# The first stage of a hybrid decoder layer: identity, silu, row sums and two bias rows rearranged

## The chip, the cores and the metric

The kernel runs on one core of a Trainium2 chip. Its engines are TensorE (PE, with its weight loads as PEld), VectorE (DVE), ScalarE (ACT), GpSimd (POOL) and SyncE (SP), which here only issues DMAs. The metric is the device time of one execution in microseconds. Changes of 0.3% and less can hardly be told from none.

## What is computed

One decoder layer on 256 tokens of 1024 features, all in float32. `c` is one row of 1024, `ada_w` is 1024 x 6144.

```python
mod = silu(c) @ ada_w + ada_b
sh1, sc1, gt1, sh2, sc2, gt2 = split(mod, 6)
h = rmsnorm(x, norm1_g) * (1 + sc1) + sh1
x = x + gt1 * hybrid_mixer(h)          # w_in: 1024 x 6144, RG-LRU and gMLP branches, merged, w_out
h = rmsnorm(x, norm2_g) * (1 + sc2) + sh2
x = x + gt2 * moe(h)                   # router: 32 experts, top 4; clamped SwiGLU experts of 1024
out = rmsnorm(x, final_g)
```

In the gMLP branch the weights `w_s` (8 groups, 128 x 128) are used as lower triangles, and a bias row `b_s` is added; the router adds `b_router`.

## The kernel before, in words

**Loads.** SBUF holds 24 slots of 128 x 2048 floats, 1 MB each. All large weights stream through them in one list of loads, which SP issues in order: `pump` issues the next load when a slot is free, `give` frees one. At most eight of SP's loads are in flight, since a load waits for the one eight before it. The list begins with the pieces of `ada_w` for `sh1` and `sc1` ("a1", six pieces: feature blocks 0, 1, 2-3, 4-5, 6, 7 as `PIECES` says) in turn with the blocks of `w_in` that go with them ("w"). Then come the rest of the mixer's weights with 16 loads of `ada_w` for the other four parts ("a2"), then 12 MB for each of 32 experts. Behind the load ("w", 6), the hook `small_loads` puts four small loads into the queue: the row `b_s` (4 KB, to one partition), the row `b_router` (128 bytes, to one partition), `w_s` and the LRU gate weights.

**Products.** All products of the mixer are made from float32 split in two parts: `split(u)` takes half a slot, ScalarE copies it rounded (the high part, line 259), and POOL or VectorE subtracts to get the low part (line 263; `ON_POOL` says which). Units 1 to 10 are subtracted on POOL, 0, 11, 12 and 14 on VectorE, and later on odd ones on POOL, even ones mostly on VectorE. `product(u)` then runs 24 matmuls: high x high, high x low part of the activations, low x high. After unit 11 the splits run four units ahead of the products.

**The first stage.** Constants first: POOL makes the identity (line 212), the strict triangle `lt` (line 215), a ramp `iota` (line 218) and clears `selX` (line 239). The rows of x are normalized into `xh` (lines 226 to 230). silu of c is made from a tanh (lines 234 to 236) and put into the columns of `selX` (`cz`). Then `transposes` turns all of xh with 16 TensorE transposes into four banks and copies these to `xT`. For each piece, `ada_rows(i)` sums the piece's `ada_w` rows weighted by silu(c): pieces 0, 1, 4, 5 (`ROWS_ON_PE`) by eight matmuls of 32 output rows on TensorE and one copy, pieces 2 and 3 by eight operations on VectorE of 128x512 (lines 339 and 341). `ada_cols(i)` finishes the sum with small matmuls against ones and adds the bias columns; `modulate(i)` applies shift and scale to xT and splits the result into `hh` and `hl`, the activations of every product. Pieces and products take turns in the order that the lines behind `n_steps = len(chunks)` write out by hand; each engine takes its instructions in that order.

**Further on.** After unit 13, `lower_triangles` masks the eight `w_s` blocks on POOL, then spreads the two bias rows to all partitions with `partition_broadcast` (lines 375 and 378), which is a custom instruction of POOL. Convolution, gates, scan and gating follow beside the products of steps 6 to 33, mainly on VectorE and ScalarE, and the 16 "a2" loads are accumulated on VectorE (lines 399 and 401). Then the router, and 32 experts one after the other.

The first pieces in the order that is written out by hand:

```python
transposes()
drop("xh")
ada_rows(0)
ada_cols(0)
split(0)
modulate(0)
```

## Time and profile before

| what | us |
|---|---|
| median of 3 runs | 1290.69 |
| lowest, highest | 1287.26, 1291.13 |
| the profiled execution | 1289.19 |
| its span in the profile | 1287.5 |
| PE busy (6667 matmuls) | 1199.5 |
| DVE busy | 554.8 |
| ACT busy | 256.7 |
| POOL busy (80 instructions) | 143.8 |

The profile holds one execution. The span runs from the first instruction to the last. The page cuts it in 40 equal slices and gives the busy share of each engine in tenths, PEclk, the granted TensorE clock in tenths of full speed, and what the DMA engines moved. The timeline lists instructions in order of time; in brackets behind a row stands how long its engine was idle before it and what released it. "issue" means that the profile shows nothing for which it waited. The windows give busy time by engine over chosen stretches.

### The profile page before, as it was taken

To read this page: it belongs to the slowest core of one execution; us is meant where nothing else is said; L and a number is where in the kernel's file an instruction comes from. 1 tells how busy PE (TensorE), PEld (TensorE's weight loads), DVE (VectorE), ACT (ScalarE), POOL (GpSimd) and SP (SyncE) were. 2 spreads that over 40 slices of the span, in tenths; PEclk is the share of its full clock that TensorE was granted. 3 is DMA by queue.
4 is the path that set the end of the run, shared out by engine and by line. 5 is a ranking of instruction groups with operands and counts; after the bars stand their busy time and mean duration, and the time that the engine had idled before them with its cause. 6 is when DMAs were issued, how large, how long until landed. Compare 5 with 4: busy or idle time off the path is not lost. (4 is left out here: it accounts for less than half of the span.)

```text
span 1287.5 us, 17398 instructions
## 1 busy us (share of the span) xinstructions
PE 1199.5 (93%) x6667; PEld 633.9 (49%) x6667; DVE 554.8 (43%) x993; ACT 256.7 (20%) x474; POOL 143.8 (11%) x80
## 2 busy tenths in 40 slices
PE   5797889999999999999999999999999999998996
PEld 4796888986444443444444444443433333433442
DVE  4586998665233333333333333333333333334324
ACT  3264633443111111111111111111111111101112
POOL 2443645531000000000000000000000000000010
PEclk8898999999999999999999999999999999999998
DMA  9964526978999999999999999999999999999960
GB/s 372 419 273 168 230 100 228 404 290 330 362 418 417 416 404 417 419 418 418 419 419 419 418 418 419 418 418 415 414 414 416 415 414 412 418 412 419 412 244 35
DMA packets 66582, 472.94 MB, mean 367 GB/s; under 512 B 7577, under 2 KB 7705, under 8 KB 10308
## 3 DMA queue, kind: packets, MB, share of 16 engines
q1 hardware_dynamic: 66100, 470.13, 89.6%
q8 instruction: 114, 1.87, 0.6%
q14 instruction: 96, 0.79, 0.2%
q0 software_dynamic: 272, 0.16, 0.0%
HBM read 469.21 MB, written 1.05 MB: 365 GB/s over the span
## 5 line engine op out<-in xcount | busy, mean ns | idle before, releaser
L268 PE MATMUL bank<-gu,gv 128*64 128x512 f32 (+1 forms) x2112 | 471.3, 597 | 13.4 <-DMA gu<-in_w_gu 7.7
L268 PEld LDWEIGHTS bank<-gu,gv 128*64 128x64 f32 (+1 forms) x2112 | 144.9, 136 | 300.1 <-issue 258.1
L268 PE MATMUL bank<-dn,tmp 128*64 128x512 f32 (+3 forms) x1120 | 240.9, 580 | 1.1 <-ACT tmp L983 0.3
L268 PEld LDWEIGHTS bank<-dn,tmp 128*64 128x64 f32 (+1 forms) x1120 | 72.5, 136 | 133.6 <-issue 119.1
L268 PEld LDWEIGHTS bank<-selX,x 128*128 128x128 f32 x1024 | 118.4, 193 | 39.4 <-DVE tmp L969 38.3
L268 PE MATMUL bank<-selX,x 128*128 128x128 f32 x1024 | 124.6, 280 | 12.1 <-PEq L1221 12.1
L995 DVE TENSOR_REDUCE wsl<-bank 128x1 f32<-128x256 f32 x33 | 14.0, 425 | 279.4 <-PE bank L994 279.4
L263 POOL TENSOR_TENSOR parts<-w,parts 128x1024 fp32r<-128x1024 f32 x40 | 117.9, 2956 | 116.7 <-ACT parts L259 83.5
L268 PE MATMUL bank<-hh,parts 128*128 128x256 f32 x640 | 122.2, 301 | 8.7 <-DVE parts L263 4.5
L970 ACT ACTIVATE tmp<-tmp 128x512 f32<-128x512 f32 (+1 forms) x34 | 20.8, 610 | 458.1 <-DVE tmp L969 458.1
L268 PEld LDWEIGHTS bank<-hh,parts 128*128 128x128 f32 x640 | 104.1, 206 | 12.3 <-DVE parts L263 4.9
L1253 POOL DMA_DIRECT2D selX<-in_rows x4 | 2.2, 545 | 952.8 <-PE bank L268 952.8
L1013 DVE TENSOR_TENSOR h<-bank,h 128x512 f32<-128x512 f32 x124 | 79.5, 683 | 47.4 <-PE bank L268 47.4
L268 PE MATMUL bank<-hl,parts 128*128 128x256 f32 x320 | 85.8, 299 | 0.0
L999 DVE SCALAR_TENSOR_TENSOR tmp<-bank,wsl,gt2h 128x512 f32<-128x512 f32 x31 | 23.3, 750 | 126.5 <-PE bank L268 126.5
L259 ACT ACTIVATE parts<-w 128x1024 fp32r<-128x1024 f32 x66 | 67.3, 1052 | 50.1 <-POOL parts L263 14.6
L827 DVE TENSOR_SCALAR gv<-bank,ab 128x128 f32<-128x128 f32 x128 | 43.7, 404 | 70.4 <-PE bank L268 70.4
L1001 ACT ACTIVATE on<-tmp 128x512 fp32r<-128x512 f32 x31 | 19.5, 630 | 263.0 <-DVE tmp L999 263.0
L268 PEld LDWEIGHTS bank<-hl,parts 128*128 128x128 f32 x320 | 62.2, 210 | 0.2 <-issue 0.2
L829 ACT ACTIVATE gv<-bank,ab 128x128 f32<-128x128 f32 x128 | 48.2, 457 | 65.6 <-PE bank L268 65.6
L263 DVE TENSOR_TENSOR parts<-w,parts 128x1024 fp32r<-128x1024 f32 x32 | 44.4, 1395 | 29.0 <-ACT parts L259 28.9
L969 DVE TENSOR_SCALAR tmp<-bank 128x512 f32<-128x512 f32 (+1 forms) x34 | 22.7, 668 | 68.0 <-PE bank L268 67.8
(228 smaller groups left out, 999.2 us busy)
## 6 DMA issues: line engine op xcount, KB each, us to landing
gu<-in_w_gu SPq DMA_DIRECT2D x256, 1024.0 KB, 19.8
dn<-in_w_dn SPq DMA_DIRECT2D x124, 1024.0 KB, 19.9
w<-in_mix SPq DMA_DIRECT2D x32, 1024.0 KB, 8.0
a<-in_mix SPq DMA_DIRECT2D x24, 1024.0 KB, 8.0
w<-in_mix SPq DMA_DIRECT2D x8, 512.0 KB, 16.3
dn<-in_w_dn_last SPq DMA_DIRECT2D x4, 768.0 KB, 19.8
x<-in_x SPq DMA_DIRECT2D x2, 512.0 KB, 4.2
wab<-in_lru_w SPq DMA_DIRECT2D x1, 1024.0 KB, 11.2
```

The source lines that it names most:

```text
L259: nc.scalar.activation(hi, w, AF.Copy)
L263: (nc.gpsimd if u in ON_POOL else nc.vector).tensor_tensor(lo, w, hi.bitcast(F32), op=OP.subtract)
L268: nc.tensor.matmul(o, a, b, start=start, stop=stop, skip_group_check=True)
L827: nc.vector.tensor_scalar(dst, src, ab[:, 1, k:k + 1], ab[:, 0, k:k + 1], op0=OP.mult, op1=OP.add)
L829: nc.scalar.activation(dst, src, AF.Identity, bias=ab[:, 0, k:k + 1], scale=ab[:, 1, k:k + 1])
L969: nc.vector.tensor_scalar(gcl, g, LIMIT, None, op0=OP.min)
L970: nc.scalar.activation(sig, gcl, AF.Sigmoid, scale=ALPHA)
L995: nc.vector.tensor_reduce(w, T[:, :256], axis=mybir.AxisListType.X, op=OP.add)
L999: nc.vector.scalar_tensor_tensor(osb, o, w, g, op0=OP.mult, op1=OP.mult)
L1001: nc.scalar.activation(dst[0], osb, AF.Copy)
L1013: nc.vector.tensor_tensor(xa[:, b, c], C[h], xa[:, b, c], op=OP.add)
L1253: nc.gpsimd.dma_start(frow[q], rows[R_FG:R_FG + 1, q * 256:(q + 1) * 256])
```

## The change

- The identity is made by VectorE: a ramp along the row by a scan, its 32x32 blocks transposed, and the two compared on the four diagonal blocks. The ramp is `iota`, so POOL no longer makes that one, nor clears selX. POOL keeps `lt`.
- `colt`, with c and the bias columns, is loaded ahead of x. silu of c and what hangs on it come ahead of the normalization. ScalarE so loads its tanh table first and its square root table second.
- `ada_rows(0)` comes ahead of the transposes, which are cut in four by bank: bank 0, then split, columns and modulation of piece 0, then banks 1 to 3. The split of unit 0 comes ahead of `ada_cols(0)`.
- All six pieces are summed by TensorE. The sums go to bank 7 for pieces 1 and 5, to bank 6 for the others.
- The two bias rows are loaded to all 128 partitions by SP's DMAs (512 KB and 16 KB). The three partition broadcasts are gone.

```diff
--- before.py
+++ after.py
@@ -35,7 +35,6 @@
 HI_ON_DVE = {27, 28, 29, 30, 31, 33}
 
 PIECES = ((0,), (1,), (2, 3), (4, 5), (6,), (7,))
-ROWS_ON_PE = (0, 1, 4, 5)
 
 GROUPS = ("ga", "gb", "va", "vb", "ua", "ub", "gra", "grb", "gsa", "gsb")
 COL0 = {"ga": 1024, "gb": 1536, "va": 3072, "vb": 3584, "ua": 2048, "ub": 2560,
@@ -160,18 +159,18 @@
     want(("dn", E - 1, 4), w_dn_last[:, 16 * WA:])
 
 
+    colt = t([128, N_COLS], "colt")
+    nc.sync.dma_start(colt, cols)
     xv = view(new("x"), TB)
     for b in range(TB):
         nc.sync.dma_start(xv[:, b], x[b * 128:(b + 1) * 128])
-    colt = t([128, N_COLS], "colt")
-    nc.sync.dma_start(colt, cols)
     R["tmp"] = new("tmp")
     tmp = [R["tmp"][:, i * 512:(i + 1) * 512] for i in range(4)]
     tms = [tmps.tile([128, 512], F32, name=f"tms{i}", tag="tmp") for i in range(2)]
     gt2h = t([128, 512], "gt2h")
     secure("xh", "xT", "wab", "ws", "acc")
     lg, mask, wt, posm = (t([128, TB, E], n) for n in ("lg", "mask", "wt", "posm"))
-    brow = wt[0:1, 0]
+    brb = t([128, E], "brb")
     gv = t([128, D], "gv")
     two = t([128, 64], "two", F32R)
     own = [t([128, 128], f"own{i}", F32R) for i in range(2)]
@@ -183,8 +182,8 @@
     wr = selX.rearrange("p (k e) -> p k e", k=KB)
 
     def small_loads():
-        nc.sync.dma_start(R["ws"][0:1, 1024:], rows[R_BS:R_BS + 1])
-        nc.sync.dma_start(brow, b_router)
+        nc.sync.dma_start(gv, rows[R_BS:R_BS + 1].to_broadcast([128, D]))
+        nc.sync.dma_start(brb, b_router.to_broadcast([128, E]))
         nc.sync.dma_start(R["ws"][:, :1024], sg_ws)
         nc.sync.dma_start(R["wab"], lru_w)
 
@@ -206,18 +205,33 @@
     ones, lt = (o.bitcast(F32) for o in own)
     iota = t([128, 128], "iota")
     eps = t([128, 1], "eps")
-    nc.vector.memset(tmp[2][:, :128], 1.0)
+    one = tmp[2][:, :128]
+    nc.vector.memset(one, 1.0)
+    nc.vector.memset(ident, 0.0)
     nc.vector.memset(eps, EPS)
-    nc.vector.tensor_copy(own[0], tmp[2][:, :128])
-    nc.gpsimd.affine_select(ident, tmp[2][:, :128], pattern=[[-1, 128]], compare_op=OP.is_equal, fill=0.0,
-                            base=0, channel_multiplier=1)
-
-    nc.gpsimd.affine_select(tmp[3][:, :128], tmp[2][:, :128], pattern=[[1, 128]], compare_op=OP.is_gt, fill=0.0,
-                            base=0, channel_multiplier=-1)
-    nc.gpsimd.tensor_copy(own[1], tmp[3][:, :128])
-    nc.gpsimd.iota(iota, pattern=[[1, 128]], base=0, channel_multiplier=0, allow_small_or_imprecise_dtypes=True)
+    nc.vector.memset(selX, 0.0)
+    nc.scalar.activation(tmp[3][:, :1], eps, AF.Tanh)
+    nc.vector.tensor_tensor_scan(iota, one, one, -1.0, op0=OP.mult, op1=OP.add)
+
+    nc.vector.transpose(tmp[1][:, :128], iota)
+    for r in range(4):
+        d = slice(32 * r, 32 * r + 32)
+        nc.vector.tensor_tensor(ident[d, d], tmp[1][d, d], iota[d, d], op=OP.is_equal)
+    nc.vector.tensor_copy(own[0], one)
 
     wsT = R["ws"][:, 1024:].rearrange("p (g t) -> p g t", g=8)
+
+
+    cs = t([128, 8], "cs")
+    nc.scalar.activation(cs, colt[:, C_C:C_C + 8], AF.Tanh, scale=0.5)
+    nc.vector.scalar_tensor_tensor(cs, cs, 1.0, colt[:, C_C:C_C + 8], op0=OP.add, op1=OP.mult)
+    nc.vector.tensor_scalar(cs, cs, 0.5, None, op0=OP.mult)
+    cz = selX.rearrange("p (k m) -> p k m", k=8)
+    nc.vector.tensor_copy(cz[:, :, 0], cs)
+
+    ab = t([128, 2, 8], "ab")
+    nc.vector.tensor_copy(ab[:, 0], colt[:, C_AB:C_AB + 8])
+    nc.vector.tensor_scalar(ab[:, 1], colt[:, C_AB + 8:C_AB + 16], 1.0, None, op0=OP.add)
 
 
     st = t([128, 8], "st")
@@ -230,18 +244,9 @@
         nc.vector.tensor_scalar(xh[:, b], xv[:, b], st[:, 4 + b:5 + b], None, op0=OP.mult)
 
 
-    cs = t([128, 8], "cs")
-    nc.scalar.activation(cs, colt[:, C_C:C_C + 8], AF.Tanh, scale=0.5)
-    nc.vector.scalar_tensor_tensor(cs, cs, 1.0, colt[:, C_C:C_C + 8], op0=OP.add, op1=OP.mult)
-    nc.vector.tensor_scalar(cs, cs, 0.5, None, op0=OP.mult)
-
-    cz = selX.rearrange("p (k m) -> p k m", k=8)
-    nc.gpsimd.memset(selX, 0.0)
-    nc.vector.tensor_copy(cz[:, :, 0], cs)
-
-    ab = t([128, 2, 8], "ab")
-    nc.vector.tensor_copy(ab[:, 0], colt[:, C_AB:C_AB + 8])
-    nc.vector.tensor_scalar(ab[:, 1], colt[:, C_AB + 8:C_AB + 16], 1.0, None, op0=OP.add)
+    nc.gpsimd.affine_select(tmp[3][:, :128], one, pattern=[[1, 128]], compare_op=OP.is_gt, fill=0.0,
+                            base=0, channel_multiplier=-1)
+    nc.gpsimd.tensor_copy(own[1], tmp[3][:, :128])
 
 
     parts = {}
@@ -311,37 +316,30 @@
 
     xT = view(R["xT"], 8)
 
-    def transposes():
-        for b in range(TB):
-            for kb in range(KB):
-                nc.tensor.transpose(B[kb // 2][:, (kb % 2) * 256 + b * 128:(kb % 2) * 256 + b * 128 + 128],
+    def transposes(p):
+        for kb in (2 * p, 2 * p + 1):
+            for b in range(TB):
+                nc.tensor.transpose(B[p][:, (kb % 2) * 256 + b * 128:(kb % 2) * 256 + b * 128 + 128],
                                     xh[:, b, kb * 128:(kb + 1) * 128], ident)
-        for p in range(4):
-            dst, src = xT[:, 2 * p:2 * p + 2], B[p].rearrange("p (k s) -> p k s", k=2)
-            if p % 2:
-                nc.vector.tensor_copy(dst, src)
-            else:
-                nc.scalar.activation(dst, src, AF.Copy)
+        dst, src = xT[:, 2 * p:2 * p + 2], B[p].rearrange("p (k s) -> p k s", k=2)
+        if p % 2:
+            nc.vector.tensor_copy(dst, src)
+        else:
+            nc.scalar.activation(dst, src, AF.Copy)
 
     g1 = t([128, 2, 8], "g1")
 
     def ada_rows(i):
 
         n = len(PIECES[i])
-        y, rk = tmp[i % 2][:, :256 * n], B[6 + i % 2][:, :256 * n]
+        y, rk = tmp[i % 2][:, :256 * n], B[7 if i in (1, 5) else 6][:, :256 * n]
         for j in range(n):
             v = view(where["a1", i, j], 8 // n)
             for kk in range(8 // n):
                 k = j * 4 + kk
-                if i in ROWS_ON_PE:
-                    mm(rk[32 * (k % 4):32 * (k % 4) + 32], cz[:, k], v[:, kk], k < 4, k >= 4)
-                elif k:
-                    nc.vector.scalar_tensor_tensor(y, v[:, kk], cs[:, k:k + 1], y, op0=OP.mult, op1=OP.add)
-                else:
-                    nc.vector.tensor_scalar(y, v[:, kk], cs[:, k:k + 1], None, op0=OP.mult)
+                mm(rk[32 * (k % 4):32 * (k % 4) + 32], cz[:, k], v[:, kk], k < 4, k >= 4)
             give()
-        if i in ROWS_ON_PE:
-            nc.scalar.activation(y, rk, AF.Copy)
+        nc.scalar.activation(y, rk, AF.Copy)
 
     def ada_cols(i):
 
@@ -365,17 +363,12 @@
     hh, hl = view(R["hh"], 8), view(R["hl"], 8)
 
     bsb = gv
-    brb = t([128, E], "brb")
 
     def lower_triangles():
         for h in range(2):
             for g in range(4):
                 nc.gpsimd.affine_select(wsn[h][:, g], wsn[h][:, g], pattern=[[-1, 128]], compare_op=OP.is_ge,
                                         fill=0.0, base=0, channel_multiplier=1)
-        nc.gpsimd.partition_broadcast(brb, brow)
-        for h in range(2):
-            c = slice(h * 512, (h + 1) * 512)
-            nc.gpsimd.partition_broadcast(bsb[:, c], R["ws"][0:1, 1024:][:, c])
 
     def spatial_weights():
         for h in range(2):
@@ -696,12 +689,14 @@
             mm_t(u, bo[g], k0, f, l, hh, hl, **kw)
 
     n_steps = len(chunks)
-    transposes()
+    ada_rows(0)
+    transposes(0)
+    split(0)
+    ada_cols(0)
+    modulate(0)
+    for p in range(1, 4):
+        transposes(p)
     drop("xh")
-    ada_rows(0)
-    ada_cols(0)
-    split(0)
-    modulate(0)
 
     def cols(i):
         ada_cols(i)
```

Where this moves instructions (names with a number are tiles: bank6 is a PSUM bank, a1_2_0 the first load of piece 2, parts0 the split of unit 0, own0 the ones, selX the columns of silu(c)).

TensorE at the start of the program, before:

```order
L317 MATMUL bank0_69<-ident_126,xh_86 128x128 x2
L317 MATMUL bank1_70<-ident_126,xh_86 128x128 x2
L317 MATMUL bank2_71<-ident_126,xh_86 128x128 x2
L317 MATMUL bank3_72<-ident_126,xh_86 128x128 x2
L317 MATMUL bank0_69<-ident_126,xh_86 128x128 x2
L317 MATMUL bank1_70<-ident_126,xh_86 128x128 x2
L317 MATMUL bank2_71<-ident_126,xh_86 128x128 x2
L317 MATMUL bank3_72<-ident_126,xh_86 128x128 x2
L268 MATMUL bank6_75<-a1_0_0_102,selX_99 32x256 x8
L268 MATMUL bank7_76<-own0_97,tmp_82 128x1 x2
L268 MATMUL bank7_76<-a1_1_0_106,selX_99 32x256 x8
```

and with the change:

```order
L273 MATMUL bank6_75<-a1_0_0_103,selX_100 32x256 x8
L322 MATMUL bank0_69<-ident_127,xh_86 128x128 x4
L273 MATMUL bank7_76<-own0_98,tmp_82 128x1 x2
L322 MATMUL bank1_70<-ident_127,xh_86 128x128 x4
L322 MATMUL bank2_71<-ident_127,xh_86 128x128 x4
L322 MATMUL bank3_72<-ident_127,xh_86 128x128 x4
L273 MATMUL bank7_76<-a1_1_0_107,selX_100 32x256 x8
```

The sums of piece 0 come first, four transposes stand ahead of the small matmuls that read the sums, and twelve behind them.

VectorE around the sums of piece 2, before:

```order
L359 TENSOR_SCALAR tmp_82<-xT_87,g1_155 128x256
L363 TENSOR_TENSOR hl_101<-tmp_82,hh_100 128x256
L341 TENSOR_SCALAR tmp_82<-a1_2_0_111,cs_146 128x512
L339 SCALAR_TENSOR_TENSOR tmp_82<-a1_2_0_111,cs_146,tmp_82 128x512 x3
L339 SCALAR_TENSOR_TENSOR tmp_82<-a1_2_1_113,cs_146,tmp_82 128x512 x4
L354 TENSOR_TENSOR g1_155<-bank7_76,ab_152 128x2x2
```

TensorE in the same place with the change, behind the small matmuls of piece 1:

```order
L273 MATMUL bank7_76<-own0_98,tmp_82 128x1 x2
L273 MATMUL bank6_75<-a1_2_0_112,selX_100 32x512 x4
L273 MATMUL bank6_75<-a1_2_1_114,selX_100 32x512 x4
L273 MATMUL bank0_69<-hh_101,parts1_225 128x256 x2
L273 MATMUL bank1_70<-hh_101,parts1_225 128x256 x2
```

The eight operations left VectorE; eight matmuls of 32x512 stand on TensorE ahead of product 1, whose operands are parts1.

POOL from the split of unit 13 on, before:

```order
L263 TENSOR_TENSOR parts13_638<-w_6_222,parts13_638 128x1024
L263 TENSOR_TENSOR parts15_658<-w_7_269,parts15_658 128x1024
L263 TENSOR_TENSOR parts17_734<-w_8_275,parts17_734 128x1024
L373 AFFINE_SELECT ws_89<-ws_89 128x128 x8
L375 ISA
L375 ISA brb_156<-wt_93 128x32
L378 ISA gv_95<-ws_89 128x512 x2
L263 ISA
L263 TENSOR_TENSOR parts19_819<-w_9_332,parts19_819 128x1024
```

and with the change:

```order
L268 TENSOR_TENSOR parts13_646<-w_6_228,parts13_646 128x1024
L268 TENSOR_TENSOR parts15_666<-w_7_275,parts15_666 128x1024
L268 TENSOR_TENSOR parts17_742<-w_8_281,parts17_742 128x1024
L370 AFFINE_SELECT ws_89<-ws_89 128x128 x8
L268 TENSOR_TENSOR parts19_824<-w_9_339,parts19_824 128x1024
```

The rows named ISA are configuration changes and custom instructions. Between the triangles and the split of unit 19 none is left.

## Rows read from the trace of the kernel before

**Rows 1.** The page's 40 slices of the span: DMA's busy tenths, and GB/s.
```profile
DMA  9964526978999999999999999999999999999960
GB/s 372 419 273 168 230 100 228 404 290 330 362 418 417 416 404 417 419 418 418 419 419 419 418 418 419 418 418 415 414 414 416 415 414 412 418 412 419 412 244 35
```

**Rows 2.** Timeline, 10 to 20 us: start, duration, engine, operation, count [idle before].
```profile
10.32 3.67 PE L317 MATMUL bank<-ident,xh 128*128 128x128 f32 x16 [10.32 <-POOL ident L212]
13.18 0.69 DVE L322 COPY xT<-bank 128x512 f32<-128x512 f32 x1 [1.47 <-PE bank L317]
13.92 1.94 PE L268 MATMUL bank<-a,selX 128*32 128x256 f32 x16
17.22 1.07 PE L268 MATMUL bank<-a,selX 128*32 128x256 f32 x16 [0.25 <-DVE g L354]
17.29 1.23 DVE L263 TENSOR_TENSOR parts<-w,parts 128x1024 fp32r<-128x1024 f32 x1
19.34 2.07 PE L268 MATMUL bank<-hh,parts 128*128 128x256 f32 x8 [1.05 <-ACT hh L361]
```

**Rows 3.** Timeline, 25 to 53 us, of TensorE and VectorE.
```profile
25.77 1.80 PE L268 MATMUL bank<-hh,parts 128*128 128x256 f32 x8 [1.48 <-ACT hh L361]
26.60 9.47 DVE L339 SCALAR_TENSOR_TENSOR tmp<-a,cs,tmp 128x512 f32<-128x512 f32 x7
36.13 1.69 PE L268 MATMUL bank<-own,tmp 128*128 128x1 f32 x8 [4.29 <-DVE tmp L339]
40.34 11.52 DVE L339 SCALAR_TENSOR_TENSOR tmp<-a,cs,tmp 128x512 f32<-128x512 f32 x7
51.91 1.05 PE L268 MATMUL bank<-own,tmp 128*128 128x1 f32 x8 [2.93 <-DVE tmp L339]
```

**Rows 4.** Line 339 (VectorE's row sums): durations in ns, minimum, median, maximum.
```profile
L339 DVE SCALAR_TENSOR_TENSOR tmp<-a,cs,tmp x14: 750/752/2774, 26.6 to 51.1; 128x512 f32<-128x512 f32 x14
```

**Rows 5.** Windows: length; busy PE, PEld, DVE, ACT, POOL; PEclk, DMA share, GB/s.
```profile
26.10:29.50 3.40, 3.40 (x19) 3.40 (x17) 3.33 (x4) 1.51 (x2) 2.76 (x1) 0.50 1.01 419
36.30:43.10 6.80, 6.80 (x33) 6.80 (x34) 4.94 (x9) 3.58 (x5) 2.64 (x1) 0.50 1.03 422
53.70:56.60 2.90, 2.90 (x16) 2.90 (x15) 1.19 (x4) 2.76 (x5) 0.99 (x1) 0.50 1.00 412
101.60:111.60 10.00, 6.21 (x15) 4.91 (x16) 3.83 (x3) 3.21 (x5) 7.43 (x3) 0.51 0.06 26
101.95:116.62 14.67, 11.23 (x37) 9.10 (x38) 4.78 (x4) 6.93 (x12) 9.09 (x3) 0.68 0.18 60
128.70:181.30 52.60, 44.37 (x328) 41.48 (x326) 51.82 (x52) 29.99 (x43) 31.32 (x12) 0.94 0.49 181
```

**Rows 6.** Timeline of POOL, 80 to 110 us.
```profile
84.28 3.01 POOL L373 TENSOR_SCALAR_AFFINE_SELECT ws<-ws 128x128 f32<-128x128 f32 x8
94.11 0.31 POOL L375 PARTITION_BROADCAST brb<-wt  x1 [6.82 <-issue]
103.00 4.67 POOL L263 TENSOR_TENSOR parts<-w,parts 128x1024 fp32r<-128x1024 f32 x2 [7.22 <-issue]
```

**Rows 7.** Timeline of TensorE, at 105 and 176 us.
```profile
105.39 0.79 PE L268 MATMUL bank<-parts,hh 128*128 128x512 f32 x1 [7.13 <-POOL parts L263]
176.81 0.58 PE L268 MATMUL bank<-ws,v 128*128 128x128 f32 x1 [4.35 <-DVE ws L410]
```

**Rows 8.** Line 122: two loads, to landing; first split of the second.
```profile
L122 SPq DMA_DIRECT2D a<-in_mix x1: 432/432/432, 2.2 to 2.2; - x1
DMA to landing us min/median/max: 7.2/7.2/7.2
L122 SPq DMA_DIRECT2D w<-in_mix x1: 328/328/328, 29.7 to 29.7; - x1
DMA to landing us min/median/max: 16.3/16.3/16.3
71.86 3.89 ACT L259 ACTIVATE parts<-w 128x1024 fp32r<-128x1024 f32 x4
```

## The prediction

> **What bounds the kernel now.** I read the page's slices first, then the timeline by engine of the mixer, then windows over the stretches that stood out. The slices, 32 us each, show two programs: from the eleventh on the DMA engines are at 9 tenths of their time or more and stay there until the last two; before that they are full for two slices and sag to 6, 4, 5, 2 and 6 tenths in the third to seventh, so there the transfers wait for slots, and slots wait for the mixer's chain [rows 1]. Whatever the mixer saves before about 200 us therefore lets all later weight loads start earlier, and comes off the end in full. Transfer engines that idle for half of five slices have room to be asked earlier.
>
> Within the mixer three things stop TensorE. First, nothing runs on it until 10.32 us, when POOL's identity is ready; the sums of piece 0 start only after the 16 transposes, at 13.92 us, and its product at 19.34 us [rows 2]. Second, the row sums of pieces 2 and 3 run on VectorE for 9.47 and 11.52 us, and TensorE waits 4.29 and 2.93 us for them; it also waits 1.48 us at 25.77 us for the first modulated block [rows 3]. One such sum of 128x512 takes 0.75 us at the median and 2.77 us at the worst [rows 4]; the long ones are those beside a POOL subtraction, which is why 7 of them take 9 to 11 us. Behind each wait the granted clock is at its lower level, 0.50: for 3.40, 6.80 and 2.90 us [rows 5]. Third, at 84.28 us POOL does the eight triangles, 3.01 us, and then three partition broadcasts, with 6.82 us of "issue" before the first and 7.22 us before its next subtraction at 103.00 [rows 6]. The subtraction it owes is late, TensorE waits 7.13 us until 105.39 us [rows 7], and from 101.60 to 111.60 us the clock stands at 0.51 while TensorE is busy for 6.21 us [rows 5].
>
> **The change, part by part.** *The start.* The weights of piece 0 are asked for at 2.2 us and land 7.2 us later, at 9.4 us [rows 8]. VectorE makes the identity, zeroes selX and writes cs into it while the loads are on their way: fourteen operations, none over 128x256, so each under half of the 0.69 us that a copy of 128x512 takes [rows 2], 5 us at most. ScalarE has its part of cs early, as colt is now the first load. So the sums run at 9.4 us instead of 13.92. Their 1.94 us end at 11.4. Four of 16 transposes that take 3.67 us follow (0.9), then a copy of one bank (0.7) and what lies in before between the end of the sums, 15.86, and the product, 19.34 us: 3.5 us, with the subtraction of 1.23 us in it, which stays on VectorE ahead of the modulation [rows 2]. That gives 16.5 us. But the product writes four banks, and VectorE now copies two of them to xT only behind the modulation: a subtraction of 0.4 and two copies of 0.69 us [rows 2], so the last bank is free at 18.3 us. The start is worth 1.0 us; 0 to 2.8 are its ends. [...]
>
> *The row sums.* 4.29 and 2.93 us of waiting go, 7.2 in all [rows 3]. Their place takes 16 matmuls of 32x512. Eight of 32x256 take 1.07 us the second time [rows 2], so eight of twice the width take some 2.15, and two pieces 4.3 us. They stand where TensorE waited for the modulated block, so the 1.48 us at 25.77 us are filled too [rows 3]. With no wait of several microseconds left between 18 and 76 us, I take it that the three stretches at half the clock go with the waits ahead of them: half of 3.40 + 6.80 + 2.90 us, or 6.55 [rows 5]. Sum: 7.2 + 1.5 + 6.55 - 4.3 = 10.9 us, with the start 12 us. If none of the clock comes back it is 5.4; with the best start it is 14. The data is there: the weights of the step behind all six sums are asked for at 29.7 us, land 16.3 us later, at 46.0, and ScalarE first splits them at 71.86 us [rows 8], after this change at about 60.
>
> *The copies and the tables.* ScalarE gets two copies of 128x512 out of PSUM, each a copy like the 0.69 us one [rows 2]; they stand behind two and three splits, while TensorE has 36 and 72 matmuls of products in front of the copies' readers. Nothing for them; without those products each would cost its 0.7 us. VectorE loses 21 us of sums; what was queued behind them there, the modulation, now waits for TensorE instead.
>
> *The broadcasts.* POOL gets back what lies between the triangles' end and its next subtraction, 103.00 - 87.29 = 15.7 us [rows 6]. On TensorE that is the wait of 7.13 us [rows 7] and half of the 6.21 us at the low clock, 3.1 [rows 5]: 10.2 us if nothing else is late. VectorE is next. From 101.95 to 116.62 us it is busy for only 4.78 of 14.67 us, because its operands were behind the same stall; 9.9 us can be closed up. From 128.7 to 181.3 us it is busy for 51.82 of 52.6 us [rows 5], and TensorE's wait of 4.35 us at 176.81 us is for VectorE [rows 7]: what counts there is how much earlier VectorE is. Three POOL subtractions, 2.33 us each by the pair of 4.67 [rows 6], were behind the stall and now fall in a stretch in which VectorE works without a gap. A two-input operation of VectorE beside one of them goes from 0.75 to 2.77 us [rows 4], so up to 7 us can be lost again. Of the 9.9 us, 2.9 to 9.9 stay; I take 7, as only some of VectorE's operations there have both inputs in SBUF.
>
> [...]
>
> *The loads.* The row of 4 KB becomes 512 KB. The queue's loads come at one MB per 2.5 us in the first two slices (the engines are full there [rows 1]), so it delays all behind it by 1.3 us, and the first of those is wanted some 8 us after it lands (next part). Nothing, and no more than 1.3 if a load were just in time. Two library changes of POOL less and two table loads of ScalarE in the other order change nothing further.
>
> **The sum.** 12 + 7 = 19 us off the profiled execution's 1289.2 us: 1270 us. That execution is 1.5 us below the median of the runs shown, 1290.69, and within their spread. By the ends, 5.4 + 2.9 and 14 + 10.2 us off, it is 1281 and 1265.
>
> **The rivals.** *The port.* POOL's regained time collides with VectorE and the second part is 2.9 us or less: 1289.2 - 12 - 2.9, or 1274 us, to 1277 us. For it: VectorE's full stretch of 52 us. Against it: POOL has 15.7 us for 7 us of work. I give it 20 in 100, with the case in it that POOL's two long waits come from something else than the broadcasts and stay elsewhere (the part is then 0; in the order of the program the custom broadcasts and the changes of POOL's library around them are all that stood between those two rows).
>
> *Transfers hide it.* DMA is full in the first two slices [rows 1]. If the mixer after 50 us were waiting for loads, the 12 us would come to nothing: 1289.2 - 7, or 1282 us. Against it: the landing at 46.0 us against the use at 71.86 [rows 8]. 8 in 100.
>
> *Slower.* The broadcast load has 128 rows of SBUF read the same 4 KB of memory, and no row here shows such a load. It stands in SP's queue ahead of the triangles' source, the gate weights and every later load. The first of those on the mixer's path is the next MB of w_in: 1.5 MB of small weights and itself behind the load that lands at 46.0 us, so 46.0 + 6.3 + 1.3 = 53.6; its split is the third of the four that take 3.89 us from 71.86 us on [rows 8], 12 us earlier after the change, at about 62. So the load must last over 9 us before anything is lost, and some 28 us (19 GB/s) before the 19 us are used up; a load of 1 MB takes 7.2 us in the full queue [rows 8]. At 40 us it would be 1270 + 31, or 1301 us. 2 in 100.
>
> *More.* VectorE's long operations of the dense stretch meet POOL less often, and the waits of TensorE in it go as well: up to 5 us more, 1260 to 1264 us. 8 in 100. That nothing moves at all, 2 in 100.
>
> **How the numbers follow.** The forecast, 1264 to 1274 us, has 60 in 100, the port 20, the transfers 8, more 8, nothing 2, slower 2. The range 1263 to 1281 us leaves out most of the transfers' case and of the better one. A measurement tells 0.3%, about 4 us, from no change. Faster by more than that: 0.94; within it 0.03; slower 0.03, with a little for what I don't see.
>
> **What would show it.** Right: the first row sums at about 9.5 us; no wait for row sums at all and a granted clock of 1.0 from about 25 to 63 us; the first split of step 6 at 58 to 62 us instead of 71.86; POOL without a gap of 6 us between the triangles and its next subtraction; TensorE's wait of 7 us gone. The port shows as VectorE operations of 2 us and more in that place, and as longer waits of TensorE for VectorE about 40 us later. Transfers show as TensorE or ScalarE waiting for DMA before 80 us. Wrong as a whole: a mixer that ends 19 us sooner, but an end that doesn't follow, because the transfer engines turn out to have no room between 100 and 300 us.

## The result, and the profile after

| what | before | after |
|---|---|---|
| median of 4 runs, us | 1290.91 | 1272.65 |
| lowest, highest | 1287.26, 1291.18 | 1271.54, 1275.08 |
| profiled execution | 1289.19 | 1272.40 |
| its span | 1287.5 | 1270.6 |

The ratio is 0.9868, with a 95% interval of 0.9845 to 0.9890: about 17 us less, where 19 were forecast (1270.0; the range was 1263 to 1281).

What the DMA engines moved in the page's slices of the kernel after, which answers to [rows 1]:

```profile
GB/s 372 416 373 232 170 171 307 325 317 346 369 415 417 409 402 418 419 419 419 418 419 419 417 419 419 419 419 418 414 419 412 417 414 413 418 411 418 415 240 35
```

The mixer asks for its weights earlier: the third slice has 373 GB/s instead of 273. The end of the program still follows the mixer's.

The first stage, from the timeline of the kernel after (start, duration, engine, operation, count, and in brackets the idle time ahead and what ended it); it answers to [rows 2, 3, 8]:

```profile
9.36 1.93 PE L273 MATMUL bank<-a,selX 128*32 128x256 f32 x16 [9.36 <-DMA a<-in_mix]
12.85 2.80 PE L322 MATMUL bank<-ident,xh 128*128 128x128 f32 x12
15.58 1.75 PE L273 MATMUL bank<-a,selX 128*32 128x256 f32 x16
17.26 1.37 PE L273 MATMUL bank<-hh,parts 128*128 128x256 f32 x8
28.34 1.07 PE L273 MATMUL bank<-a,selX 128*32 128x512 f32 x8 [0.29 <-DMA a<-in_mix]
30.83 1.93 PE L273 MATMUL bank<-a,selX 128*32 128x512 f32 x8 [1.42 <-DMA a<-in_mix]
60.45 3.89 ACT L264 ACTIVATE parts<-w 128x1024 fp32r<-128x1024 f32 x4
```

The first split of step 6 comes at 60.45 us instead of 71.86, 11.4 us earlier. No wait for a row sum is left. (The profile counts each of these sums twice: a row with x8 has four.) But the second load of piece 3 (row 30.83) lands only when TensorE has waited 1.42 us for it, and the four sums behind it take 1.93 us where the four ahead of it took 1.07.

Windows of the kernel after (length; busy PE, PEld, DVE, ACT, POOL; PEclk, DMA share, GB/s), which answer to [rows 5]; the last one is the router, between the first product of the mask and the first of expert 0. PEclk is a mean over the stretch; in windows of 0.4 us from 10 to 110 and from 280 to 320 us it is 1.00 or 0.50 in 346 of 350 here and in 339 of 350 in the kernel before:

```profile
30.00:33.00 3.00, 2.17 (x9) 0.51 (x10) 0.14 (x1) 1.56 (x2) 2.31 (x1) 0.61 1.00 411
101.60:111.60 10.00, 8.44 (x53) 6.96 (x52) 8.94 (x30) 7.79 (x16) 1.00 (x1) 1.00 0.87 314
284.77:295.17 10.40, 10.40 (x60) 10.19 (x60) 3.16 (x17) 1.92 (x7) 0.00 (x0) 0.67 1.01 425
```

The same stretch of the router in the kernel before:

```profile
303.38:312.38 9.00, 9.00 (x61) 8.63 (x61) 3.16 (x17) 1.93 (x7) 0.00 (x0) 0.81 1.02 425
```

POOL in the kernel after, which answers to [rows 6], and TensorE's wait for VectorE that answers to the second of [rows 7]:

```profile
72.86 3.00 POOL L370 TENSOR_SCALAR_AFFINE_SELECT ws<-ws 128x128 f32<-128x128 f32 x8
76.85 3.44 POOL L268 TENSOR_TENSOR parts<-w,parts 128x1024 fp32r<-128x1024 f32 x1 [0.98 <-ACT parts L264]
...
157.72 1.01 PE L273 MATMUL bank<-ws,v 128*128 128x128 f32 x3 [4.40 <-DVE ws L403]
```

From the triangles' end at 75.86 us to POOL's next subtraction pass 1.0 us instead of 15.7. TensorE's wait of 7.13 us is gone; that of 4.35 us for VectorE is still there, as 4.40.

**Where the time went.** One product gives the mixer's progress: the second group of the product with the recurrent branch begins at 222.32 us before and at 203.25 us after. That is 19.07 us, what was forecast. Then 0.5 us are lost ahead of the router's transposes (277.59 us, 296.20 before), where TensorE waits 0.45 us for VectorE, and 1.4 us in the router, whose 61 matmuls take 10.40 us at a granted clock of 0.67 instead of 9.00 us at 0.81. The expert phase takes 0.3 us longer than before, and its end is 16.9 us earlier.

The change also moved which operations of VectorE meet a subtraction of POOL: a meeting, here, is an operation of VectorE that lasts longer where such a subtraction runs beside it (the accumulation at 92.24 us takes 4.48 us beside POOL's subtraction from 91.08 to 94.56 us, the one at 88.84 us 2.34 us with none beside it). Where the prediction and the expectations say port, the traces show these durations, and not what the two engines share. These are its seven accumulations of 128x2048 in the mixer's middle (minimum, median, maximum in ns), of after and of before:

```profile
L392 DVE SCALAR_TENSOR_TENSOR acc<-a,cs,acc x7: 2337/4466/4491, 84.8 to 126.6; 128x2048 f32<-128x2048 f32 x7
```

```profile
L399 DVE SCALAR_TENSOR_TENSOR acc<-a,cs,acc x7: 2341/2345/4493, 96.2 to 145.7; 128x2048 f32<-128x2048 f32 x7
```

Four of the seven now take 4.5 us and one did before: 25.6 us in sum against 18.6. Other operations of VectorE went the other way. Here are three of them and the scan, of after and then of before:

```profile
103.39 0.16 DVE L455 TENSOR_SCALAR lg<-colt 128x8 f32<-128x8 f32 x1
113.89 2.31 DVE L262 CAST parts<-w 128x1024 fp32r<-128x1024 f32 x2
145.53 3.58 DVE L561 TENSOR_SCALAR v<-v,mv,rs 128x1024 f32<-128x1024 f32 x2
149.03 4.59 DVE L523 TENSOR_TENSOR_SCAN p<-a,xc 128x256 f32<-128x256 f32 x4
```

```profile
120.03 2.37 DVE L462 TENSOR_SCALAR lg<-colt 128x8 f32<-128x8 f32 x1
132.74 4.75 DVE L257 CAST parts<-w 128x1024 fp32r<-128x1024 f32 x2
164.67 5.70 DVE L568 TENSOR_SCALAR v<-v,mv,rs 128x1024 f32<-128x1024 f32 x2
170.29 2.42 DVE L530 TENSOR_TENSOR_SCAN p<-a,xc 128x256 f32<-128x256 f32 x4
```

The three lost 2.2 + 2.4 + 2.1 = 6.8 us (before rounding) and the scan gained 2.2. In all VectorE pays 7.0 + 2.2 - 6.8 = 2.4 us more for its meetings with POOL.

### The profile page after: what moved, and what is told of

Same layout as the page of the kernel before. It is cut to its first block, busy times and chain, and to the rows that moved or that the text cites. A ratio compares the mean times of both kernels' runs of the same rounds, so it can differ in the third digit from the quotient of the medians.

```text
span 1270.6 us, 17442 instructions
## 1 busy us (share of the span) xinstructions
PE 1196.4 (94%) x6699; PEld 627.4 (49%) x6699; DVE 537.8 (42%) x985; ACT 257.4 (20%) x477; POOL 138.3 (11%) x74
## 5 line engine op out<-in xcount | busy, mean ns | idle before, releaser
L273 PE MATMUL bank<-gu,gv 128*64 128x512 f32 (+1 forms) x2112 | 471.3, 597 | 13.4 <-DMA gu<-in_w_gu 7.4
L268 POOL TENSOR_TENSOR parts<-w,parts 128x1024 fp32r<-128x1024 f32 x40 | 115.2, 2888 | 109.7 <-ACT parts L264 67.7
L273 PE MATMUL bank<-hh,parts 128*128 128x256 f32 x640 | 117.7, 292 | 6.1 <-DVE parts L268 3.7
L273 PEld LDWEIGHTS bank<-hh,parts 128*128 128x128 f32 x640 | 100.2, 197 | 12.2 <-DVE parts L268 4.1
L273 PE MATMUL bank<-hl,parts 128*128 128x256 f32 x320 | 83.2, 288 | 0.0
L264 ACT ACTIVATE parts<-w 128x1024 fp32r<-128x1024 f32 x66 | 67.1, 1051 | 52.6 <-POOL parts L268 16.9
L273 PEld LDWEIGHTS bank<-hl,parts 128*128 128x128 f32 x320 | 59.2, 198 | 0.2 <-issue 0.2
L392 DVE SCALAR_TENSOR_TENSOR acc<-a,cs,acc 128x2048 f32<-128x2048 f32 x14 | 53.7, 3836 | 0.0
## 6 DMA issues: line engine op xcount, KB each, us to landing
dn<-in_w_dn_last SPq DMA_DIRECT2D x4, 768.0 KB, 19.3
```

The lines of the kernel that those rows point to most:

```text
L264: nc.scalar.activation(hi, w, AF.Copy)
L268: (nc.gpsimd if u in ON_POOL else nc.vector).tensor_tensor(lo, w, hi.bitcast(F32), op=OP.subtract)
L273: nc.tensor.matmul(o, a, b, start=start, stop=stop, skip_group_check=True)
L392: nc.vector.scalar_tensor_tensor(R["acc"], w, s_, R["acc"], op0=OP.mult, op1=OP.add)
```

## The experiments

Two questions were tested first: how the gain divides among the three parts, and what in the broadcasts costs the time. The later runs went after the two things that the trace after showed, the meetings and the late load. The comparison is with the kernel before, run on the same chip (medians 1289.85 to 1290.07 us in the three sessions); 1272.65 is the kernel after, which was not run again beside them, so a difference of a microsecond or two from it is not told from none. Each kernel has one profile.

**Row sums alone (rows_only).** The kernel before with

```diff
-ROWS_ON_PE = (0, 1, 4, 5)
+ROWS_ON_PE = (0, 1, 2, 3, 4, 5)
-        y, rk = tmp[i % 2][:, :256 * n], B[6 + i % 2][:, :256 * n]
+        y, rk = tmp[i % 2][:, :256 * n], B[7 if i in (1, 5) else 6][:, :256 * n]
```

> Only the row sums of pieces 2 and 3 move to TensorE; start and broadcasts are those of the kernel before. Theory A (the waits for the row sums and the low clock behind them were the stage's loss): no wait for VectorE's sums, and the first split of step 6 at 61 to 62.5 us instead of 71.86; of the 11.4 us that the whole change gains there, 9 to 11 come from this part, and the kernel takes 1279 to 1282 us. Rival B (the start carries half of the stage's gain): the split at about 66 us, 1285 us. Rival C (loads bound the stage, so that whatever moves it is cut off at the landing of piece 3): the same split as with the whole change, 60.5 us.

Measured: 1278.64 us, ratio 0.9913 (0.9894 to 0.9931). Its timeline:

```profile
22.73 0.50 PE L268 MATMUL bank<-own,tmp 128*128 128x1 f32 x4
23.17 1.92 PE L268 MATMUL bank<-a,selX 128*32 128x512 f32 x16
30.33 2.04 PE L268 MATMUL bank<-a,selX 128*32 128x512 f32 x16
59.47 3.89 ACT L259 ACTIVATE parts<-w 128x1024 fp32r<-128x1024 f32 x4
```

The split comes at 59.47 us, earlier than theory A's 61 and earlier than with the whole change, so neither A's number nor C's fits. Of the 12.4 us, 1.1 were there before any moved instruction had run: the columns of piece 1 begin at 22.73 us, and at 23.79 us before. Up to there the code is the same, and the granted clock is not: 1.00 from 13 to 25 us here, 0.87 from 13 to 26 us before. (From the first transpose to those columns it is 1.95 us less; the transposes begin 0.89 us later here, at 11.21 us.) The remaining 11.3 us are theory A's. The eight sums of piece 3 run in 2.04 us without any wait for a load, because they come 2 us later than in the kernel after.

**Bias rows alone (loads_only).** The kernel before with

```diff
-        nc.sync.dma_start(R["ws"][0:1, 1024:], rows[R_BS:R_BS + 1])
-        nc.sync.dma_start(brow, b_router)
+        nc.sync.dma_start(gv, rows[R_BS:R_BS + 1].to_broadcast([128, D]))
+        nc.sync.dma_start(brb, b_router.to_broadcast([128, E]))
...
-        nc.gpsimd.partition_broadcast(brb, brow)
-        for h in range(2):
-            c = slice(h * 512, (h + 1) * 512)
-            nc.gpsimd.partition_broadcast(bsb[:, c], R["ws"][0:1, 1024:][:, c])
```

> Only the two bias rows come spread by loads; the first stage is that of the kernel before. Theory A: POOL's two long waits go with the three broadcasts, TensorE's wait of 7.13 us goes, and the bias product of TensorE that begins at 140.05 us in the kernel before begins 7 to 9 us earlier; 1282 to 1285 us. Rival B (the port takes most of it back): 3 us or less at that product, 1288 us. Rival C (the waits have another cause): POOL's gaps of about 7 us stay, and the time with them, 1291 us.

Measured: 1281.93 us, ratio 0.9939 (0.9917 to 0.9961). The timeline of POOL and TensorE:

```profile
84.18 3.00 POOL L372 TENSOR_SCALAR_AFFINE_SELECT ws<-ws 128x128 f32<-128x128 f32 x8
88.14 3.48 POOL L263 TENSOR_TENSOR parts<-w,parts 128x1024 fp32r<-128x1024 f32 x1 [0.96 <-ACT parts L259]
131.30 1.88 PE L268 MATMUL bank<-ws,own 128*128 128x512 f32 x4
```

Its accumulations, in ns as above:

```profile
L394 DVE SCALAR_TENSOR_TENSOR acc<-a,cs,acc x7: 2342/4470/4497, 96.1 to 138.0; 128x2048 f32<-128x2048 f32 x7
```

The bias product begins 8.75 us earlier (140.05 before), and 7.65 us are left at the product with the recurrent branch. Theory A holds. The median accumulation is at 4.47 us as in the kernel after, so this part brought the meetings: without POOL's stall its subtractions fall beside them.

**The start alone (start_only).** The kernel after with the other two parts taken back:

```diff
+ROWS_ON_PE = (0, 1, 4, 5)
...
-        nc.sync.dma_start(gv, rows[R_BS:R_BS + 1].to_broadcast([128, D]))
+        nc.sync.dma_start(R["ws"][0:1, 1024:], rows[R_BS:R_BS + 1])
...
+                elif k:
+                    nc.vector.scalar_tensor_tensor(y, v[:, kk], cs[:, k:k + 1], y, op0=OP.mult, op1=OP.add)
...
+        nc.gpsimd.partition_broadcast(brb, brow)
```

> Only the start is rearranged; pieces 2 and 3 are summed on VectorE and the rows are spread on POOL as in the kernel before. Theory A: the product of piece 0 starts at 17.3 us instead of 19.34, and 1 to 2 us of it reach the first split of step 6 (70 to 71 us); 1289 to 1290 us, which a time alone can hardly tell from no change. Rival B (VectorE's sums absorb it, since they wait for POOL's port and not for their data): the split stays at 71.9 us. Rival C (it carries half of the first stage): the split at 66 us, 1285 us.

Measured: 1289.37 us (10 runs), ratio 0.9994 (0.9982 to 1.0007). Its timeline:

```profile
17.60 1.24 PE L274 MATMUL bank<-hh,parts 128*128 128x256 f32 x8
32.95 1.86 PE L274 MATMUL bank<-own,tmp 128*128 128x1 f32 x8 [5.02 <-DVE tmp L344]
48.90 1.86 PE L274 MATMUL bank<-own,tmp 128*128 128x1 f32 x8 [3.83 <-DVE tmp L344]
70.18 3.89 ACT L265 ACTIVATE parts<-w 128x1024 fp32r<-128x1024 f32 x4
```

1.7 us reach the split, 1.1 us the product with the recurrent branch, and the time can't tell the rest from nothing. TensorE waits 8.85 us for VectorE's two sums instead of 7.22: it is earlier and waits for the same engine.

**One broadcast back (one_broadcast).** The kernel after with the router's bias, 32 elements a row, spread by POOL again:

```diff
-        nc.sync.dma_start(brb, b_router.to_broadcast([128, E]))
+        nc.sync.dma_start(wt[0:1, 0], b_router)
...
+        nc.gpsimd.partition_broadcast(brb, wt[0:1, 0])
```

> The changed kernel with one of the three partition broadcasts back on POOL, the smallest one (32 elements a row, the router's bias), behind the triangles; the two large ones stay loads. Theory A (the cost is POOL's change to the broadcast's code and back, whatever is broadcast): the two waits of about 7 us are back whole, TensorE waits some 7 us for POOL again, and the kernel is 5 to 9 us slower than the changed one, 1278 to 1282 us. Rival B (the cost goes with the broadcasts' number or size): under 1 us, 1273 us.

Measured: 1278.79 us, 6.1 us above the kernel after; the ratio to before is 0.9917 (0.9897 to 0.9938), outside the interval of the kernel after. POOL's timeline:

```profile
71.46 2.99 POOL L370 TENSOR_SCALAR_AFFINE_SELECT ws<-ws 128x128 f32<-128x128 f32 x8
80.84 0.31 POOL L372 PARTITION_BROADCAST brb<-wt  x1 [6.39 <-DMA w<-in_mix]
89.36 4.66 POOL L268 TENSOR_TENSOR parts<-w,parts 128x1024 fp32r<-128x1024 f32 x2 [8.22 <-DVE acc L393]
```

One broadcast of 0.31 us brings back both pauses, 6.39 us ahead of it and 8.22 us behind it, and a wait of TensorE of 6.3 us. The releasers named there are taken to be other engines' events that happen to fall last; the pauses are those of [rows 6]. Theory A: the price goes with the two pauses (14.6 us of POOL together), not with the broadcast. What POOL does in them, whether it changes its code as the theory says or its library as the prediction does, no run shows.

The start of this kernel is that of the kernel after, and TensorE's rows there differ from those above:

```profile
12.61 1.51 PE L322 MATMUL bank<-ident,xh 128*128 128x128 f32 x12
16.50 0.50 PE L273 MATMUL bank<-hh,parts 128*128 128x256 f32 x2
17.57 1.10 PE L273 MATMUL bank<-hh,parts 128*128 128x256 f32 x6 [0.56 <-DVE xT L326]
```

The twelve transposes take 1.51 us instead of 2.80, the sums of piece 1 behind them 1.07 instead of 1.75, and the product begins at 16.50 us.

**Without the start (no_start).** The edits of rows_only and of loads_only together in the kernel before.

> The changed kernel without its start: row sums on TensorE and rows by loads as there, but identity, silu and the order of the first sums as in the kernel before. Theory A (the start's 2 us end in the wait for piece 3's loads): the product of piece 0 begins at 19.3 to 19.8 us, no wait for a load at 28 to 31 us, the first split of step 6 at 59 to 60 us, so as early as with the start or earlier, and 1270 to 1272.5 us. Rival B (the start carries its 1 to 2 us): the split at 61.5 us or later, 1273.5 to 1275 us.

Measured: 1272.02 us, ratio 0.9862 (0.9846 to 0.9878). Timeline:

```profile
18.78 1.21 PE L268 MATMUL bank<-hh,parts 128*128 128x256 f32 x8 [1.05 <-ACT hh L361]
29.34 2.08 PE L268 MATMUL bank<-a,selX 128*32 128x512 f32 x16
58.49 3.89 ACT L259 ACTIVATE parts<-w 128x1024 fp32r<-128x1024 f32 x4
```

Theory A: the product of piece 0 starts 1.5 us later than in the kernel after, the sums of piece 3 find their data there, and the split is 2 us earlier. Part of that is not the edits': the columns of piece 1 begin at 21.74 us here and at 23.79 before, on the same code (granted clock 1.00 from 13 to 25 us, 0.86 before), and the product came ahead of the 19.3 us expected because the sums of piece 0 took 1.45 us instead of 1.94. But one_broadcast, row_twice and port_all, which have the start and lose no clock behind the load, have the split at 59.03, 58.92 and 58.94 us, and rows_only and no_start, without it, at 59.47 and 58.49. In the time, too, the start is worth nothing that these runs can tell. Row sums and loads, 11.25 and 7.96 us by themselves, make 18.05 together, so they add up but for 1.2 us.

**Piece 3's loads earlier (early_load).** The kernel after with one line in the order of the loads:

```diff
+    order[8:11] = order[9:11] + order[8:9]
```

> The changed kernel with both loads of piece 3 (1 MB each) ahead of the second half of the first gate weights (512 KB). Theory A (the start's lead of 2 us ends in the wait for piece 3's second load, 1.42 us at 30.83 us, and TensorE's clock is at 0.61 from 30 to 33 us behind it): the load lands 1.25 us sooner, the wait falls to about 0.2 us, and the first split of step 6 comes at 57.5 to 59.5 us instead of 60.45; 1270 to 1272 us. Rival B (the gate weights become late instead): the split at 60 us or later, TensorE or ScalarE waits for w between 33 and 45 us, 1273 us or more.

Measured: 1270.31 us, ratio 0.9849 (0.9832 to 0.9865). Timeline:

```profile
29.81 1.06 PE L274 MATMUL bank<-a,selX 128*32 128x512 f32 x8 [0.45 <-DMA a<-in_mix]
57.94 3.89 ACT L265 ACTIVATE parts<-w 128x1024 fp32r<-128x1024 f32 x4
```

The wait falls from 1.42 to 0.45 us, the sums behind it run in 1.06 instead of 1.93, and the split is 2.5 us earlier. Some 1.1 us of that are the load's: one_broadcast, which waits 1.43 us and loses no clock, has the split at 59.03 us; the other 1.4 are the clock that fell in the profile of the kernel after. The trace bears out theory A. The time does not show it: 2.3 us are gained, but the intervals of the two kernels overlap.

**The row loaded twice (row_twice).** The kernel after with the broadcast load of 512 KB issued a second time, right behind the first (the data are the same).

> The changed kernel with the 512 KB broadcast load of the bias row issued twice, one behind the other. Theory A (it is hidden): no new wait for a load on TensorE or ScalarE, the loads behind it land 1.3 us later, the time stays within 1.5 us of 1272.65 us. Rival B (the queue behind it is on the path): 1.3 us or more slower with a wait for w or wab between 40 and 80 us; or, if such a load is far slower than 400 GB/s, many us slower.

Measured: 1272.36 us, ratio 0.9861 (0.9843 to 0.9879). SP's timeline:

```profile
47.11 0.33 SPq L186 DMA_DIRECT2D gv<-in_rows  x1
47.48 0.43 SPq L187 DMA_DIRECT2D brb<-in_b_router  x1
```

The delay was ten times the expected one: the second load waited until the first, issued at 33.24 us, had landed, and what follows was issued at 47.48 us instead of 34.56, the next load of w_in at 48.97 instead of 40.88. Even so nothing became late. Theory A holds by a wider margin than was meant.

**Subtractions off POOL (port_two, port_four, port_all).** The kernel after with, in turn, half steps (units) 23 and 25, 28 to 31, and 21 to 37 taken out of the set that POOL subtracts; this is the third:

```diff
-ON_POOL = set(range(1, 11)) | {28, 30} | {u for u in range(12, 68) if u % 2}
+ON_POOL = (set(range(1, 11)) | {28, 30} | {u for u in range(12, 68) if u % 2}) - set(range(21, 38))
```

> The changed kernel with the subtractions of half steps 23 and 25, which stand on POOL at 91.08 and 98.89 us there, on VectorE. Theory A (the port: an accumulation of 128x2048 takes 4.48 us beside a POOL subtraction and 2.34 us alone, and two of them meet just these two): VectorE pays 1.21 us more for each subtraction and gets back 2.14 us for each accumulation, so it is 1.9 us earlier from 104 us on, and up to that much reaches TensorE's waits behind 128 us: 1271 to 1272.5 us against 1272.65. Rival B (VectorE is short of time whoever shares the port): its two more operations make it 2.4 us later, 1274 to 1275 us.

> The changed kernel with the subtractions of half steps 28 to 31 on VectorE; on POOL they stand as two pairs of 7.1 us, at 115.68 and 126.14 us, each beside an accumulation (4.48 us instead of 2.34) and two operations of 128x512 (3.45 us together). Theory A (the port): VectorE pays 4.8 us and gets back 2 x 2.1 and 2 x about 1.9 us, 8 us, so it is 3 us earlier behind 135 us; TensorE's waits of 1.15 and 1.24 us for POOL go, since the parts are ready sooner; 1268 to 1271 us. Rival B: VectorE is 4.8 us later and TensorE's wait of 4.40 us at 157.72 us grows by as much, 1276 to 1278 us.

> The changed kernel with all of POOL's subtractions of half steps 21 to 37 on VectorE (eleven), so that no POOL subtraction stands beside VectorE between 83 and 152 us. Theory A (the port): eleven times 1.2 us more, 13 us, against some six meetings of 2.1 us and the two pairs with operations of 128x512, 16 to 18 us: VectorE 3 to 5 us earlier at 157 us, 1268 to 1271 us. Rival B (the port matters only for some of them, so the many that met nothing cost in full): VectorE 5 us or more later, 1275 to 1280 us.

Measured: 1271.97, 1267.62 and 1265.32 us, ratios 0.9850 (0.9828 to 0.9872), 0.9821 (0.9801 to 0.9841) and 0.9812 (0.9796 to 0.9828). The accumulations in port_all (minimum, median, maximum in ns):

```profile
L392 DVE SCALAR_TENSOR_TENSOR acc<-a,cs,acc x7: 2345/2346/2347, 83.3 to 124.5; 128x2048 f32<-128x2048 f32 x7
```

The sum of VectorE that ends TensorE's wait, in the kernel after and in port_all, and that wait in port_all:

```profile
157.01 0.66 DVE L403 TENSOR_TENSOR ws<-bank,ws 128x512 f32<-128x512 f32 x1
149.17 0.66 DVE L403 TENSOR_TENSOR ws<-bank,ws 128x512 f32<-128x512 f32 x1
149.88 0.49 PE L273 MATMUL bank<-ws,v 128*128 128x128 f32 x2 [2.89 <-DVE ws L403]
```

Rival B of each run wanted a slower kernel, and none is. Two subtractions are within the error; four and eleven are not. The product with the recurrent branch begins 1.7 us earlier with two and 2.7 us earlier with four. In port_all VectorE does eleven operations more, and TensorE's product at 157.72 us starts at 149.88: 7.8 us earlier, of which 1.5 are the first stage (58.94 instead of 60.45 us). All seven accumulations take 2.35 us. From the first of them to that sum VectorE needs 65.9 us (83.30 to 149.17) instead of 72.2 (84.78 to 157.01): 6.4 us less, which with the 1.5 is the whole. Theory A holds, though its 3 to 5 us were too few. In that stretch VectorE is busy for 63.3 us instead of 70.6 while it does eleven subtractions more, some 13 us of work, so the meetings that went had cost it some 20 us, not 16 to 18. Between 85 and 160 us TensorE waits 2.4 us for POOL in the kernel after and not at all here.

**Both, and all of them (port_early, all_early).** The eleven subtractions and the earlier loads; then the same with half steps 21 to 67, so that POOL has none behind the first stages:

```diff
+ON_POOL = (set(range(1, 11)) | {28, 30} | {u for u in range(12, 68) if u % 2}) - set(range(21, 68))
...
+    order[8:11] = order[9:11] + order[8:9]
```

> The changed kernel with the eleven subtractions of half steps 21 to 37 on VectorE and piece 3's loads earlier, both at once. Theory A (two different stretches, so both gains add up): 7.3 and 2.3 us off 1272.65, 1262 to 1264 us. Rival B (the second is swallowed, because VectorE's chain from 84 us on doesn't start from TensorE): 1265 us, as with the subtractions alone.

> The same with all later subtractions of the mixer (half steps 21 to 67) on VectorE as well, so that POOL has none of them. Theory A (accumulations of 4.0 us beside POOL fall to 2.35 us in the second half too, but TensorE waits there for parts only 6.8 us in all): 0 to 3 us better than the last, 1260 to 1263 us. Rival B (behind 160 us VectorE is late for other operations when it has fourteen subtractions more): 2 us or more worse, 1265 us and up, with longer waits of TensorE for parts from VectorE.

Measured: 1262.61 us, ratio 0.9789 (0.9773 to 0.9805), and 1256.34 us, ratio 0.9740 (0.9724 to 0.9756). The page's row of busy time of all_early (us, share of the span, instructions):

```profile
PE 1191.3 (95%) x6699; PEld 626.2 (50%) x6699; DVE 528.6 (42%) x1011; ACT 258.2 (21%) x477; POOL 61.8 (5%) x48
```

Its accumulations on VectorE from 150 to 262 us (busy us, mean ns, then idle time ahead):

```profile
L393 DVE SCALAR_TENSOR_TENSOR acc<-a,cs,acc 128x2048 f32<-128x2048 f32 x7 | 17.4, 2491 | 0.0
```

The same row of the page of the kernel after:

```profile
PE 1196.4 (94%) x6699; PEld 627.4 (49%) x6699; DVE 537.8 (42%) x985; ACT 257.4 (20%) x477; POOL 138.3 (11%) x74
```

The accumulations of port_early from 150 to 262 us:

```profile
L393 DVE SCALAR_TENSOR_TENSOR acc<-a,cs,acc 128x2048 f32<-128x2048 f32 x7 | 26.0, 3710 | 0.0
```

The VectorE of all_early has 26 operations more than that of the kernel after and is busy for 9.2 us less. The two gains of port_early add up, 10.0 us against 7.3 and 2.3, as theory A said, but its interval overlaps that of port_all, so the time does not show the second by itself. The last step gave 6.3 us where 0 to 3 were expected: from port_early to all_early the second seven accumulations fall from 26.0 to 17.4 us, and TensorE's waits for parts behind 85 us from 8.7 to 2.4. all_early beats both kernels, by 16 us the one after and by 34 us the one before.

## Why the prediction was right, and where it was not

*The bound.* That what the mixer gains before 200 us comes off the end held but for 2.2 us: the mixer's 19.07 us became 16.9. Of the rest 1.9 us are in TensorE's work behind that product, up to the router's end, and 0.3 in the expert phase, so the transfers took 0.3 at most.

*The start: the step "worth 1.0 us" failed.* The first sums ran at 9.36 us (9.4 forecast), but the product at 17.26 instead of 16.5. The high part of its activations was ready at 16.42 us, as the step has it; TensorE was not. From 9.36 us to the product it has no wait, and the twelve transposes of 2.80 us and the sums of piece 1 of 1.75 us stand ahead of the product: work that the step left out. In one_broadcast, where both took less, the product did begin at 16.50 us, and then waited 0.56 us for a bank, as the step expected of the banks. In the kernel after the product was still 2.1 us ahead of before, more than the 1.0 forecast. The lead ended at 30.83 us in the wait for piece 3's second load, and in this execution the clock fell to 0.61 behind it (in one_broadcast the same wait of 1.43 us cost no clock, and its split comes at 59.03 us). The sentence "The data is there" was checked on the load behind all six sums alone; the one that mattered is in the middle, and beside the other two parts nothing of the lead is left at the split (start_only, where that load is not waited for, keeps 1.7 us of it). no_start and early_load show it from both sides. So the rival "transfers hide it" was true of this part, and of no other.

*The row sums: 10.9 us forecast, 11.3 at the split in rows_only once the lead that was there before is taken off, 11.25 by the time.* The terms hold one by one: the eight sums of a piece took 1.92 and 2.04 us in rows_only, 4.0 against 4.3 for the pair, and with that the step's own sum is 11.3. From 25 to 63 us TensorE there is busy without a gap at a clock of 1.00. In the kernel after it is busy for 36.3 of these 38 us at 0.96, for the load and the clock behind it.

*The broadcasts: 7 us forecast, 7.65 in loads_only at the product with the recurrent branch, 7.96 by the time, and 6.1 when one comes back.* The mechanism was one that the rows only suggested, that both pauses belong to the broadcasts; one_broadcast shows it. Of the 9.9 us of VectorE that could close up, the step took off 2.9 for meetings with POOL; the meetings cost 2.4 more than before, so 7.5 should be left. From its first accumulation to the start of the sum that ends TensorE's wait of 4.40 us, VectorE needs 72.2 us after (84.78 to 157.01) and 79.9 before (96.21 to 176.10): 7.7 us less. The size was right, but not the reason that the step gave for it (that only some operations have both inputs in SBUF): meetings were exchanged, 9 us new for 7 us old. Operations with one input meet POOL too, as the rows of the kernel before show: 2.37 us instead of 0.16 for the TENSOR_SCALAR of 128x8.

*The port.* The rival had the place and the price, some 2 us a meeting. What it missed is that the kernel before paid for meetings too, at other operations, and lost those. In the traces an accumulation takes 2.35 us alone and some 4.48 beside a POOL subtraction, about the sum of the two (2.4 us for POOL's). What the prediction left out is what follows: VectorE does the subtraction itself in 1.22 us (port_all), less than the 2.1 us that a meeting of an accumulation costs it, and port_all is 7.3 us faster than the kernel after.

*The loads: nothing, as forecast.* The row landed 13.9 us after its issue and nobody waited; row_twice put 13 us on the queue right behind it and 8 on the next load of w_in, and still nobody did. The rival "slower" had it that a load of over 9 us would cost time; this one took longer and delayed nothing, since the queue issued its next load 1.25 us behind it (34.56 us).

*What was not in the sum.* 1.4 us in the router, by the clock, 0.5 us in a wait for VectorE ahead of it, and 0.3 us in the expert phase, whose cause is open.

## What to carry to other kernels

When a stage gets faster, look up every load inside it, not only the last: a lead that ends in front of one load is worth nothing. A helper engine whose operations make those of a busy one last longer costs more than it takes off as soon as a meeting is dearer than the work moved (here 2.1 us against 1.22); count the meetings in the durations of one and the same operation, minimum against median. The custom operation here was priced by the two pauses around it (6.39 and 8.22 us around 0.31 us in one_broadcast), so removing two of three gained nothing: with all three, rows_only takes 1278.64 us, and with one, one_broadcast takes 1278.79.

## What the runs showed of the hardware that was not expected

The router's 61 matmuls between the first product of the mask and the first of expert 0 are the same in all fourteen profiles, with no wait in them. They took 9.00 and 8.89 us at a granted clock of 0.81 (before, loads_only), 10.4 to 10.7 at 0.67 or 0.68 (ten kernels) and 12.0 at 0.57 (row_twice, all_early). all_early, the fastest, has the slowest router (its window, columns as above):

```profile
266.94:278.96 12.02, 12.02 (x60) 11.76 (x61) 3.17 (x17) 2.08 (x7) 0.00 (x0) 0.57 0.93 391
```

So 3 us of a span can come from the clock on the same instructions, and the kernel before had the better clock in its profile. With one profile for each kernel it is not shown whether that changes from execution to execution or goes with the kernel. At the start it goes with more than the code: up to 22 us the code of before, loads_only, rows_only and no_start is the same, and from the first transpose to the columns of piece 1 the first two take 13.4 to 13.5 us (clock 0.87), the others 11.5 (clock 1.00).
